# A new first stage for a gated-convolution layer: the first token tile ahead of the second, ScalarE for the second tile's tokens, and a hand-set order for a few loads and low parts

## The chip, the core and the metric

The kernel runs on one core of one Trainium2 chip. The metric is the device time of one execution in microseconds (us). Five engines work beside each other and meet through semaphores: TensorE (PE in the profile; its weight loads are listed apart as PEld) multiplies matrices, VectorE (DVE) and ScalarE (ACT) do elementwise work, GpSimd (POOL) does a little of it, and SyncE (SP) issues nearly all the loads from HBM. All loads run on the core's 16 DMA engines.

## The reference

One layer of a decoder, for 256 tokens of width D = 2048, with an inner width E = 4096, all in fp32:

```python
h = rmsnorm(x, norm_g)
mod = silu(c) @ ada_w + ada_b              # (1, 3 * 2048): shift, scale, gate
shift, scale, gate = split(mod, 3)
h = h * (1 + scale) + shift
b_gate, c_gate, v, g = split(h @ w_in, 4)  # w_in is 2048 x 16384
u = causal_depthwise_conv(c_gate * v, conv_w)      # width 3
y = (b_gate * u * silu(g)) @ w_out         # w_out is 4096 x 2048
out = rmsnorm(x + gate * y, final_g)
```

The weights are read once. `w_in` is 128 MB, `w_out` 32 MB and `ada_w` 48 MB; the multiplications of `h @ w_in` and `y @ w_out` make up nearly all of TensorE's work.

## The kernel before

**Precision.** Every fp32 operand of the large products is split in two: a high part (ScalarE casts it to the matmul type, `split_hi`) and a low part (VectorE subtracts the high part from the original, `split_lo`). A product is then three matmuls: high by high, high weights by low tokens, low weights by high tokens. So every weight tile passes through ScalarE and then VectorE before TensorE can use it, and so do the tokens: `hh_[k]` and `hl_[k]` are the high and low parts of token tile k (128 of the 2048 features, by 256 tokens).

**Token tiles.** x is normalised, turned by TensorE and scaled by `norm_g` into `xs`. Tile k is then modulated with the shift and scale of its 128 features (`mod`), which need all 2048 rows of two column blocks of `ada_w`. The 16 tiles are made in 8 groups of two. The first group is made in the first stage, which is written out in a fixed order on each engine (`in_order`, lines 202 to 434). For each later group `ada_piece` loads eight pieces of two 256 KB loads each; `ada_sums` adds each piece on VectorE to a sum (line 476 for the first row block, 478 for the others); `ada_done` lets TensorE turn the sums (line 486), VectorE reduces them, and `modulate` adds the biases (line 326) and makes the tokens: `high_tokens` on ScalarE (line 330), `low_tokens` on VectorE (lines 334 and 337). Below, piece 1 to 8 are those of the second group (tiles 2 and 3).

**The first stage.** The 16 row blocks of the first group's columns are loaded (line 233) and summed partly on TensorE (blocks 1, 11, 13 and 15: `sum0` with the row block as it is) and partly on VectorE (line 415, into `gv0`); TensorE then adds `gv0` over its partitions with a column of ones (`sum0(None, ...)`), once for the shift half and once for the scale half. Row block 15 is shared: its shift half goes to TensorE, its scale half to VectorE. One VectorE instruction adds the biases for both tiles (line 420 through 326). Then the tokens: both high parts on ScalarE, tile 0's low part on VectorE (334, 337), tile 1's by ScalarE (line 429) and GpSimd (line 433). Between them stand the high and low parts of the first weights (`raw0`, two blocks of 128 x 512).

**Passes.** `part(ch, q, k0, k1, seed)` multiplies token tiles k0 to k1 with the columns of chunk ch, quarter q of `w_in` and gathers the result in a PSUM bank; ScalarE copies it to `acc` (line 518). `plan()` fixes the order of passes and pieces with a model of its own. Counting them in that order, passes 1 to 13 use token tiles 0 and 1 alone (24 matmuls each), passes 14 to 16 tiles 0 to 3 (48 each). Pass 1 uses `raw0`; passes 2 to 13 load 512 KB each and passes 14 to 16 load 1 MB each (line 540). In most passes the matmuls go block by block: high by high, high by low tokens, low by high; so the low part of the weights is needed at the third matmul.

**Order.** In the program the pieces and passes alternate: pass 2, pass 3, piece 1, pass 4, piece 2, pass 5, pass 6, piece 3, pass 7, piece 4, pass 8, piece 5, pass 9, and so on; piece 1 of the third group stands between passes 13 and 14. Behind the first stage a scheduler of the compiler sets the order on every engine and in SP's queue, from these priorities, the dependencies and the places that are free. `behind(last)` adds an edge: what is traced inside goes after the named instructions on its engine. `later(GIVE)` gives the sums a lower priority. There are three places of 2048 columns each for raw weights, high parts and low parts (a 512 KB load takes half a place), and four for pieces. Passes 6 and 7 take the place of `raw0`.

**Small loads.** The convolution's weights (`rows2`, line 585) are loaded by GpSimd's queue; the load is traced at the tenth pass and goes behind the last GpSimd instruction of the first stage (`behind(ended)`).

Of the kernel before, what the change touches and what calls it, by code (L numbers as in the profile page):

```python
# [8 lines left out]
F32 = mybir.dt.float32  # L9
F32R = mybir.dt.float32r  # L10
AF = mybir.ActivationFunctionType
ALU = mybir.AluOpType

P = 128
# [3 lines left out]
KT = D // P  # L18
# [6 lines left out]
CT = 4  # L25
NCH = 4
NS = CT * NCH
ADA = [2] * 8
# [89 lines left out]
def short_conv_layer(ctx: ExitStack, tc: tile.TileContext, x, c, norm_g, ada_w, ada_b, w_in, conv_w, w_out, final_g, out):  # L118
    nc = tc.nc
# [58 lines left out]
    @contextmanager  # L178
    def behind(last):

        traced = nc.cur_bb.bb.instructions
        n = len(traced)
        yield
        for ins in list(traced[n:]):
            if ins.engine in last:
                tc.add_manual_dep(ins, last[ins.engine], after, reason="behind")
# [13 lines left out]
    ended = {}  # L200
# [23 lines left out]
    adas = ada_w[0].rearrange("(k p) (s f) -> p k s f", p=P, s=3)  # L224
    NK0 = ADA[0]
    first_ada = []
    for n, (j, kk) in enumerate(((0, 4), (4, 4), (8, 4), (12, 2), (14, 1), (15, 1))):
        at = w_tile(("lo", "hi")[n % 2], "at0")[:, : kk * 2 * NK0 * P]
        at = at.rearrange("p (k s f) -> p k s f", k=kk, s=2)
# [11 lines left out]
    ones = const.tile([P, 1], F32, tag="ones", name="ones")  # L241
# [29 lines left out]
    bias = vec[:, KT : 3 * KT].rearrange("p (s k) -> p s k", s=2)  # L271
# [6 lines left out]
    for t in range(TT):  # L278
        for dh in range(2):
# [3 lines left out]
            else:  # L283
                nc.vector.scalar_tensor_tensor(
                    out=junk[:, t], in0=xt[t][dh], scalar=1.0, in1=xt[t][dh], op0=ALU.mult, op1=ALU.mult,
# [14 lines left out]
    def tokens(k, part):  # L300
        return (hT[:, k] if k < KB else hT2[:, k - KB])[:, part * T : (part + 1) * T]

    hh_ = [tokens(k, 0) for k in range(KT)]
    hl_ = [tokens(k, 1) for k in range(KT)]
    xs = [slot([P, CT, T], f"xs{j}") for j in range(KT // CT)]
# [15 lines left out]
    mod = const.tile([P, 2, KT], F32, tag="mod", name="mod")  # L321

    def add_biases(k0, nk, sums):
        ks = slice(k0, k0 + nk)
        sums = sums.rearrange("p (s k) -> p s k", s=2)
        nc.vector.tensor_tensor(out=mod[:, :, ks], in0=sums, in1=bias[:, :, ks], op=ALU.add)

    def high_tokens(k):
        hf = xs[k // CT][:, k % CT, :]
        nc.scalar.activation(hh_[k], hf, AF.Identity, bias=mod[:, 0, k : k + 1], scale=mod[:, 1, k : k + 1])  # L330

    def low_tokens(k):
        hf = xs[k // CT][:, k % CT, :]
        nc.vector.tensor_scalar(
            out=hf, in0=hf, scalar1=mod[:, 1, k : k + 1], scalar2=mod[:, 0, k : k + 1], op0=ALU.mult, op1=ALU.add
        )
        nc.vector.tensor_tensor(out=hl_[k], in0=hf, in1=hh_[k].bitcast(F32), op=ALU.subtract)

    def modulate(k0, nk, sums):

        add_biases(k0, nk, sums)
        for k in range(k0, k0 + nk):
            high_tokens(k)
            low_tokens(k)

    last_low = [None]

    def hi_tile():
        return w_tile("hi", "hi", F32R)
# [4 lines left out]
    def split_hi(raw, n, hi=None):  # L354
        hi = hi_tile() if hi is None else hi
        nc.scalar.copy(hi[:, :n], raw[:, :n])  # L356
        return hi

    def split_lo(raw, n, hi, lo_tag="lo", lo=None):
        lo = lo_tile(lo_tag) if lo is None else lo  # L360
        last_low[0] = nc.vector.tensor_tensor(  # L361
            out=lo[:, :n], in0=raw[:, :n], in1=hi[:, :n].bitcast(F32), op=ALU.subtract
        )
        return hi, lo
# [19 lines left out]
    sums0 = psum.tile([P, 512], F32, tag="sm", name="sum0", bufs=2)  # L384
    gv0 = adap.tile([P, 2, 2 * P], F32, tag="gv", name="gv0")[:, :, 0 : NK0 * P]
    for dh in range(2):
        for t in range(TT):
            nc.scalar.activation(xt[t][dh], xt[t][dh], AF.Copy, scale=rstd[:, t : t + 1])
    def sum0(k, rows, col, halves=(0, 1)):


        for o in range(2 * NK0):
            if o // NK0 in halves:
                nc.tensor.matmul(
                    sums0[:, o * P : (o + 1) * P], rows[:, o // NK0, (o % NK0) * P : (o % NK0 + 1) * P],
                    col.to_broadcast([P, P]),
                    start=k == ON_PE[0] and o == 0, stop=k is None, skip_group_check=True,
                )

    for k in range(KT):  # L400
        c_k = silu_c[:, k : k + 1]
        at, gv = first_ada[k], gv0
        if k in ON_PE:
            if k == 11:
                for j in range(3):
                    keep_x(j, turn_x(j))
                tp_3 = turn_x(3)
            sum0(k, at, c_k, (0,) if k == KT - 1 else (0, 1))
            if k < KT - 1:
                continue  # L410
            at, gv = at[:, 1], gv0[:, 1]
        if k == 0:
            nc.vector.tensor_scalar_mul(gv, at, c_k)
        else:
            nc.vector.scalar_tensor_tensor(out=gv, in0=at, scalar=c_k, in1=gv, op0=ALU.mult, op1=ALU.add)
    for half in range(2):
        sum0(None, gv0, ones[:, 0:1], (half,))
    blocks0 = [raw0[:, k * CT * P : (k + 1) * CT * P] for k in range(NK0)]
    hi0 = [split_hi(b, CT * P) for b in blocks0]
    add_biases(0, NK0, sums0.rearrange("p (o f) -> p o f", o=2 * NK0)[:, :, 0])  # L420
    pieces0 = []
    for k in range(NK0):
        high_tokens(k)
    for k in range(NK0):
        if k == 0:
            pieces0.append(split_lo(blocks0[k], CT * P, hi0[k]))
            low_tokens(k)
        else:
            nc.scalar.activation(
                xs[0][:, k, :], xs[0][:, k, :], AF.Identity, bias=mod[:, 0, k : k + 1], scale=mod[:, 1, k : k + 1]  # L430
            )
            pieces0.append(split_lo(blocks0[k], CT * P, hi0[k]))
            nc.gpsimd.tensor_tensor(out=hl_[k], in0=xs[0][:, k, :], in1=hh_[k].bitcast(F32), op=ALU.subtract)
    pinned.close()

    def conv(ct, u, cv):
# [17 lines left out]
    def ada_piece(k0, nk, piece):  # L454
        w = nk * P
        kk = ASLOT // (2 * w)
        if piece == 0:
            sums[k0] = adap.tile([P, 2, 2 * P], F32, tag="gv", name="gv")
        gv = sums[k0][:, :, 0:w]
        j = piece * kk  # L460
        at = adap.tile([P, ASLOT], F32, tag="at", name="at", bufs=4)
        at4 = at.rearrange("p (k s f) -> p k s f", k=kk, s=2)
        for s in range(2):
            nc.sync.dma_start(at4[:, :, s, :], adas[:, j : j + kk, s, k0 * P : k0 * P + w])  # L464
        with later(GIVE):
            ada_sums(j, kk, at4, gv)
        if j + kk == KT:
            with later(-LEAD):
                ada_done(k0, nk, gv)
# [39 lines left out]
            product(bank[:, m, :], hi[:, o], lo[:, o], k, i, begins and i == 0, m % 2 == 0, 2 in parts and k == k1 - 1 and (m, i) == terms[-1])  # L509

    last_mm = [None]
    kept, added = [], []

    def keep(ch, q, k0, bank, seed=False):
        if k0 == 0 or seed:
# [6 lines left out]
    def part(ch, q, k0, k1, seed):  # L522


        col = q * E + ch * CT * P
        step = SLOT // (CT * P)
        first = k0
        bank = psum.tile([P, CT, T], F32, tag="mm", name="mm_s")
        if seed:
            nc.scalar.copy(bank, acc[ch, q])  # L530
        if pieces0:
            for k in range(NK0):
                chunk_products(bank, *pieces0[k], 0, k, k0, k1, late=True)
            pieces0.clear()
            k0 = NK0
        for s0 in range(k0, k1, step):
            sk = min(step, k1 - s0)
            n = sk * CT * P
            raw, hi, lo = places(n)
            nc.sync.dma_start(  # L540
                raw[:, :n].rearrange("p (k f) -> p k f", k=sk),
                w_in[0, s0 * P : (s0 + sk) * P, col : col + CT * P].rearrange("(k p) f -> p k f", p=P),
            )
            at = len(acc) if k0 == 0 else KT
            with behind(ended if at < 3 else kept[at - 3] if at < 9 else {}):
                split_hi(raw, n, hi)
            with behind(ended if at < 3 else added[at - 3] if at < 5 else {}):
                split_lo(raw, n, hi, lo=lo)
            for parts in ((0, 1), (2,)) if 0 < len(acc) < 3 else ((0, 1, 2),):
                for i in range(sk):  # L550
                    chunk_products(bank, hi, lo, i * CT * P, s0 + i, k0, k1, seed, parts=parts)
        if len(acc) == 1:
            with behind(ended):
                keep_x(3, tp_3)
        keep(ch, q, first, bank, seed)
        kept.append({ins.engine: ins.name for ins in nc.cur_bb.bb.instructions[-1:]})
# [109 lines left out]
    for ct in range(NS, NCT, 2):  # L666
        for q in QUARTERS:
            bank = psum.tile([P, CT, T], F32, tag="mm", name="mm_b")[:, 0:2]
            col = q * E + ct * P
            for kp in range(0, KT, KP):  # L670
# [6 lines left out]
                for m in range(2):  # L677
                    for i in range(KP):
                        k = kp + i
                        o = slice((i * 2 + m) * P, (i * 2 + m + 1) * P)  # L680
# [174 lines left out]
    halves = [wide_bank("mm_o") for _ in range(2)]  # L855
# [89 lines left out]
```

## Time and profile before

| | |
|---|---|
| median of 3 runs | 903.15 us (902.76 to 903.26) |
| the profiled execution | 903.37 us, of which 901.6 us are the span of its instructions |
| granted TensorE clock, mean | 0.997 |
| HBM read, written | 224.49 MB, 2.10 MB |
| TensorE's matmuls | 6997 |

A row of the timeline gives the start and the busy time in us, the engine, the line of the kernel, the operation, "output<-inputs" with their shapes, and how many of them were merged; in square brackets stands the idle time of the engine before it and what ended that. A "q" behind an engine marks its queue: a row of SPq is the issue of a load, and the transfer lands some us later. Windows give the busy time of each engine in a stretch, then the granted clock, the mean share of the 16 DMA engines that was busy (it can exceed 1, since a packet's time counts in full where packets overlap) and the GB/s.

### The profile page before, as it was taken

How to read it: one execution, taken by the hardware profiler on the slowest of the kernel's cores; microseconds unless marked ns; L12 is line 12 of the kernel's file. 1: busy time of each engine (PE TensorE's matmuls, PEld its weight loads, DVE VectorE, ACT ScalarE, POOL GpSimd, SP SyncE). 2: the span in 40 equal slices, each digit the busy share in tenths (PEclk: the TensorE clock that was granted, in tenths of full speed). 3: DMA queues.
4: the chain of work that ended last, by engine and by line, in shares of the span. 5: the costliest groups of instructions: out<-in, count | busy, mean ns of one | idle time of the engine just before them, and what ended most of it. 6: DMA issues, size and time to landing. Idle time of an engine off the chain costs nothing.

```text
span 901.6 us, 16416 instructions
## 1 busy us (share of the span) xinstructions
PE 887.4 (98%) x6997; PEld 850.6 (94%) x6997; DVE 675.3 (75%) x665; ACT 484.9 (54%) x429; POOL 84.8 (9%) x96
## 2 busy tenths in 40 slices
PE   7999999999999999999999999999999999999996
PEld 4899999999999999999999999999999988888885
DVE  5889989888888867765775678565555568879886
ACT  6768866665548856644443434444434445554543
POOL 0000000000000042024224302420000000000000
PEclk9999999999999999999999999999999999999998
DMA  9999999999998588687978898866666476673662
GB/s 307 365 369 368 368 315 348 356 369 352 351 326 289 165 277 250 192 257 229 295 227 247 256 289 269 240 198 197 201 193 188 141 284 222 199 275 123 203 234 94
DMA packets 159610, 235.01 MB, mean 261 GB/s; under 512 B 6900, under 2 KB 105284, under 8 KB 159152
## 3 DMA queue, kind: packets, MB, share of 16 engines
q1 hardware_dynamic: 156368, 226.52, 76.7%
q0 software_dynamic: 3040, 7.39, 2.8%
q8 instruction: 55, 0.90, 0.4%
q14 instruction: 19, 0.16, 0.1%
q10 hardware_dynamic: 128, 0.04, 0.0%
HBM read 224.49 MB, written 2.10 MB: 251 GB/s over the span
## 4 chain that ended last, share of the span: by engine, by line
PE 95%; DMA 3%; SPq 0%; ACT 0%; DVE 0%; issue 0%; ACTq 0%; DVEq 0%
PE mm_b L496 39%; PE mm_s L496 37%; PE mm_w L738 7%; PE mm_o L738 7%; PE mm L738 4%; DMA at<-in_ada_w_dram 2%; DMA x<-in_x_dram 1%; PE tp_g L486 0%; DVE lo L361 0%; SPq L464 0%; ACT hi L356 0%; ACT acc L518 0%; SPq L540 0%; SPq L218 0%; ACT big L852 0%
## 5 line engine op out<-in xcount | busy, mean ns | idle before, releaser
L496 PE MATMUL mm_s<-hT,hi 128*128 128x256 f32 x2048 | 348.4, 277 | 1.1 <-ACT hT L330 1.1
L496 PE MATMUL mm_b<-hT,hi 128*128 128x256 f32 x2048 | 348.2, 276 | 0.0
L496 PEld LDWEIGHTS mm_s<-hT,hi 128*128 128x128 f32 x2048 | 307.2, 188 | 1.3 <-ACT hT L330 1.3
L496 PEld LDWEIGHTS mm_b<-hT,hi 128*128 128x128 f32 x2048 | 308.2, 188 | 0.0
L496 PE MATMUL mm_b<-hT,lo 128*128 128x256 f32 x1024 | 282.8, 276 | 0.0
L496 PE MATMUL mm_s<-hT,lo 128*128 128x256 f32 x1024 | 280.2, 277 | 0.8 <-DVE lo L361 0.8
L356 ACT CAST hi<-raw 128x2048 fp32r<-128x2048 f32 (+1 forms) x66 | 123.7, 1875 | 193.5 <-PE mm_b L496 156.7
L361 DVE TENSOR_TENSOR lo<-raw,hi 128x2048 fp32r<-128x2048 f32 (+1 forms) x66 | 150.4, 2280 | 99.9 <-ACT hi L356 99.3
L496 PEld LDWEIGHTS mm_b<-hT,lo 128*128 128x128 f32 x1024 | 192.2, 188 | 0.0
L496 PEld LDWEIGHTS mm_s<-hT,lo 128*128 128x128 f32 x1024 | 190.7, 188 | 1.2 <-DVE lo L361 1.2
L361 DVE TENSOR_TENSOR lo<-raw_s,hi 128x2048 fp32r<-128x2048 f32 (+1 forms) x80 | 149.5, 1877 | 35.1 <-ACT hi L356 34.6
L356 ACT CAST hi<-raw_s 128x2048 fp32r<-128x2048 f32 (+1 forms) x80 | 124.2, 1558 | 58.2 <-PE mm_s L496 47.2
L478 DVE SCALAR_TENSOR_TENSOR gv<-at,silu_c,gv 128x512 f32<-128x512 f32 x105 | 78.5, 748 | 7.6 <-DMA at<-in_ada_w_dram 5.9
L518 ACT COPY acc<-mm_s 128x1024 f32<-128x1024 f32 x54 | 54.7, 1013 | 39.4 <-PE mm_s L496 39.2
L361 DVE TENSOR_TENSOR lo<-raw_o,hi 128x2048 fp32r<-128x2048 f32 x22 | 50.4, 2290 | 23.4 <-ACT hi L356 23.4
L356 ACT CAST hi<-raw_o 128x2048 fp32r<-128x2048 f32 x22 | 42.0, 1908 | 46.4 <-PE mm_w L738 12.6
L738 PE MATMUL mm_w<-hi,y 128*128 128x512 f32 x184 | 58.8, 389 | 0.0
L634 POOL TENSOR_TENSOR gacc<-gacc,z 128x512 f32<-128x512 f32 x28 | 44.7, 1597 | 116.2 <-DMA z<-gacc 116.2
L738 PE MATMUL mm_o<-hi,y 128*128 128x512 f32 x176 | 55.3, 389 | 0.0
L628 DVE SCALAR_TENSOR_TENSOR gacc<-at_g,silu_c,gacc 128x512 f32<-128x512 f32 x60 | 45.8, 764 | 8.2 <-DMA at_g<-in_ada_w_dram 7.2
L632 POOL DMA_DIRECT2D z<-gacc x28 | 15.6, 556 | 330.5 <-DVE acc L569 283.9
L738 PEld LDWEIGHTS mm_w<-hi,y 128*128 128x128 f32 x184 | 34.5, 188 | 7.2
(154 smaller groups left out, 689.4 us busy)
## 6 DMA issues: line engine op xcount, KB each, us to landing
raw<-in_sc_w_in_dram SPq DMA_DIRECT2D x64, 1024.0 KB, 5.8
raw_s<-in_sc_w_in_dram SPq DMA_DIRECT2D x47, 1024.0 KB, 8.3
raw_o<-in_sc_w_out_dram SPq DMA_DIRECT2D x32, 1024.0 KB, 5.3
at<-in_ada_w_dram SPq DMA_DIRECT2D x126, 256.0 KB, 7.9
raw_s<-in_sc_w_in_dram SPq DMA_DIRECT2D x33, 512.0 KB, 7.2
at_g<-in_ada_w_dram SPq DMA_DIRECT2D x32, 512.0 KB, 8.1
x<-in_x_dram SPq DMA_DIRECT2D x4, 512.0 KB, 6.3
big<-in_x_dram SPq DMA_DIRECT2D x2, 1024.0 KB, 8.2
```

Of the source, the lines that this page charges most:

```text
L356: nc.scalar.copy(hi[:, :n], raw[:, :n])
L361: last_low[0] = nc.vector.tensor_tensor(out=lo[:, :n], in0=raw[:, :n], in1=hi[:, :n].bitcast(F32), op=ALU.subtract)
L478: nc.vector.scalar_tensor_tensor(out=gv, in0=at4[:, i], scalar=c_k, in1=gv, op0=ALU.mult, op1=ALU.add)
L496: mm = last_mm[0] = nc.tensor.matmul(dst, w, h[k], start=begins and left, stop=ends, skip_group_check=True)
L518: nc.scalar.copy(acc[ch, q], bank)
L628: nc.vector.scalar_tensor_tensor(out=ga, in0=at3[:, i, :], scalar=s, in1=ga, op0=ALU.mult, op1=ALU.add)
L632: nc.gpsimd.dma_start(turned[0 : P - away], ga[away:P])
L634: nc.gpsimd.tensor_tensor(out=ga, in0=ga, in1=turned, op=ALU.add)
L738: nc.tensor.matmul(dst, y[a], b, start=opens and i == 0, stop=ends and i == 2, skip_group_check=True)
```

## The change

There are four edits.

1. The shared row block 15 of the first stage is divided by token tile and no longer by shift and scale: TensorE takes tile 0's part of both, VectorE tile 1's. `sum0` gets a list of tiles in place of halves, the sums with ones are made tile by tile, and the biases are added tile by tile (`first_bias`).
2. The tokens of the first group: tile 0's high part is made by VectorE, in one instruction that follows its bias; tile 0's float tokens, and both of tile 1's forms, by ScalarE (`first_tokens`); both low parts by VectorE. GpSimd makes none. The casts and low parts of the first weights alternate with them, tile by tile.
3. The loads of piece 3 go behind the load of pass 6, those of piece 4 behind the load of pass 7 (`loads`).
4. The low part of pass 14 goes behind the biases of the second group, the low part of pass 15 behind the last low part of that group's tokens (`made`).

```diff
     def modulate(k0, nk, sums):
 
         add_biases(k0, nk, sums)
+        made.append({ins.engine: ins.name for ins in nc.cur_bb.bb.instructions[-1:]})
         for k in range(k0, k0 + nk):
             high_tokens(k)
             low_tokens(k)
+        made.append({ins.engine: ins.name for ins in nc.cur_bb.bb.instructions[-1:]})
...
-    def sum0(k, rows, col, halves=(0, 1)):
+    def sum0(k, rows, col, tiles=range(NK0)):
...
-            if o // NK0 in halves:
+            if o % NK0 in tiles:
...
-            sum0(k, at, c_k, (0,) if k == KT - 1 else (0, 1))
+            sum0(k, at, c_k, (0,) if k == KT - 1 else range(NK0))
             if k < KT - 1:
                 continue
-            at, gv = at[:, 1], gv0[:, 1]
+            at, gv = at[:, :, P : NK0 * P], gv0[:, :, P : NK0 * P]
...
-    for half in range(2):
-        sum0(None, gv0, ones[:, 0:1], (half,))
     blocks0 = [raw0[:, k * CT * P : (k + 1) * CT * P] for k in range(NK0)]
-    hi0 = [split_hi(b, CT * P) for b in blocks0]
-    add_biases(0, NK0, sums0.rearrange("p (o f) -> p o f", o=2 * NK0)[:, :, 0])
+    hi0 = []
+
+    def first_bias(k):
+        sum0(None, gv0, ones[:, 0:1], (k,))
+        both = sums0.rearrange("p (s k f) -> p s k f", s=2, k=NK0)[:, :, k, 0]
+        nc.vector.tensor_tensor(out=mod[:, :, k], in0=both, in1=bias[:, :, k], op=ALU.add)
+
+    def first_tokens(k, out):
+        nc.scalar.activation(out, xs[0][:, k, :], AF.Identity, bias=mod[:, 0, k : k + 1], scale=mod[:, 1, k : k + 1])
+
     pieces0 = []
+    first_bias(0)
+    nc.vector.tensor_scalar(
+        out=hh_[0], in0=xs[0][:, 0, :], scalar1=mod[:, 1, 0:1], scalar2=mod[:, 0, 0:1], op0=ALU.mult, op1=ALU.add
+    )
     for k in range(NK0):
-        high_tokens(k)
-    for k in range(NK0):
-        if k == 0:
-            pieces0.append(split_lo(blocks0[k], CT * P, hi0[k]))
-            low_tokens(k)
-        else:
-            nc.scalar.activation(
-                xs[0][:, k, :], xs[0][:, k, :], AF.Identity, bias=mod[:, 0, k : k + 1], scale=mod[:, 1, k : k + 1]
-            )
-            pieces0.append(split_lo(blocks0[k], CT * P, hi0[k]))
-            nc.gpsimd.tensor_tensor(out=hl_[k], in0=xs[0][:, k, :], in1=hh_[k].bitcast(F32), op=ALU.subtract)
+        hi0.append(split_hi(blocks0[k], CT * P))
+        if k:
+            first_tokens(k, hh_[k])
+        first_tokens(k, xs[0][:, k, :])
+        pieces0.append(split_lo(blocks0[k], CT * P, hi0[k]))
+        if k + 1 < NK0:
+            first_bias(k + 1)
+        nc.vector.tensor_tensor(out=hl_[k], in0=xs[0][:, k, :], in1=hh_[k].bitcast(F32), op=ALU.subtract)
...
         for s in range(2):
-            nc.sync.dma_start(at4[:, :, s, :], adas[:, j : j + kk, s, k0 * P : k0 * P + w])
+            with behind(loads[piece + 2] if k0 == ADA[0] and piece in (2, 3) else {}):
+                nc.sync.dma_start(at4[:, :, s, :], adas[:, j : j + kk, s, k0 * P : k0 * P + w])
...
+            loads.append({ins.engine: ins.name for ins in nc.cur_bb.bb.instructions[-1:]})
             at = len(acc) if k0 == 0 else KT
             with behind(ended if at < 3 else kept[at - 3] if at < 9 else {}):
                 split_hi(raw, n, hi)
-            with behind(ended if at < 3 else added[at - 3] if at < 5 else {}):
+            with behind(ended if at < 3 else added[at - 3] if at < 5 else made[at - 13] if 13 <= at < 15 else {}):
                 split_lo(raw, n, hi, lo=lo)
```

More of the change, by code (lines that the diff above doesn't have):

```diff
@@ L344, in modulate @@
             low_tokens(k)
-    last_low = [None]
+        made.append({ins.engine: ins.name for ins in nc.cur_bb.bb.instructions[-1:]})
+    last_low, made = [None], []
     def hi_tile():
@@ L511, in short_conv_layer @@
     last_mm = [None]
-    kept, added = [], []
+    kept, added, loads = [], [], []
     def keep(ch, q, k0, bank, seed=False):
```

## The prediction

> **What bounds the kernel now.** I read the page's head first, then windows cut by stage, then the chain of waits.
>
> ```profile
> span 901.6 us, 16416 instructions
> PE 887.4 (98%) x6997; PEld 850.6 (94%) x6997; DVE 675.3 (75%) x665; ACT 484.9 (54%) x429; POOL 84.8 (9%) x96
> ```
>
> ```profile
> 9.00:25.00 16.00, 14.08 (x81) 9.94 (x79) 12.94 (x24) 10.70 (x21) 0.00 (x0) 1.00 1.07 353
> 25.00:42.00 17.00, 16.19 (x137) 15.80 (x138) 14.05 (x17) 14.16 (x18) 1.53 (x2) 1.00 1.06 363
> 42.00:62.00 20.00, 20.00 (x179) 20.00 (x178) 17.60 (x20) 14.86 (x16) 0.00 (x0) 1.00 1.07 369
> ```
>
> TensorE is the bound of the kernel as a whole (98%), so a gain can only come from where it is not yet full: up to 42 us. In the windows it is full from 42 us on, while the DMA engines are already full from 9 us (shares 1.07, 1.06, 1.07). So the start is a race between a stream of bytes of fixed length and TensorE, and what a load can bring forward depends on where it stands in that stream.
>
> ```profile
> 23.91 8.01 DMA at<-in_ada_w_dram
> ...
> 32.71 1.23 DVE lo L361
> ...
> 36.80 1.02 ACT acc L518
> 37.88 1.06 ACT hi L356
> 38.97 1.24 DVE lo L361
> ...
> 57.17 10.79 PE mm_s L496 x95
> ```
>
> ```profile
> 33.33 0.39 PE L496 MATMUL mm_s<-hT,hi 128*128 128x256 f32 x2
> 33.98 0.39 PE L496 MATMUL mm_s<-hT,lo 128*128 128x256 f32 x1 [0.27 <-DVE lo L361]
> ...
> 39.33 0.39 PE L496 MATMUL mm_s<-hT,hi 128*128 128x256 f32 x2
> 40.24 0.39 PE L496 MATMUL mm_s<-hT,lo 128*128 128x256 f32 x1 [0.53 <-DVE lo L361]
> ...
> 62.36 0.39 PE L496 MATMUL mm_s<-hT,hi 128*128 128x256 f32 x2
> 62.59 0.28 PE L496 MATMUL mm_s<-hT,lo 128*128 128x256 f32 x1
> ```
>
> The chain that ends last does not pass through the first products at all: it runs over a load of piece 2 (23.91), a low part (32.71), a copy, a cast and a low part (36.80 to 40.2), and from there over TensorE alone. TensorE's pace is 10.79/95 = 0.114 us a matmul. Two stalls stand behind the first product. In pass 4 (from 33.33) two matmuls take 0.23 and the third comes after 0.65: 0.42 lost; in pass 6 (39.33 to 40.24) 0.68 is lost. Each costs 0.1 more in refilling, so 0.5 and 0.8. With what the first product can gain, that is all there is to win. Pass 14 (62.36 to 62.59) runs at full pace; I come back to it.
>
> **Edits 1 and 2, the first stage.** Its rows:
>
> ```profile
> 21.11 2.06 DVE L415 SCALAR_TENSOR_TENSOR gv<-at,silu_c,gv 128x512 f32<-128x512 f32 x3 [0.45 <-DMA at<-in_ada_w_dram]
> 22.70 1.23 PE L394 MATMUL sum<-ones,gv 128*128 128x128 f32 x8
> 23.10 1.36 ACT L356 CAST hi<-raw 128x512 fp32r<-128x512 f32 x2 [1.72 <-DVE gv L415]
> 23.97 0.16 DVE L326 TENSOR_TENSOR mod<-sum,vec 128x4 f32<-128x4 f32 x1 [0.80 <-PE sum L394]
> 24.05 0.69 DVE L361 TENSOR_TENSOR lo<-raw,hi 128x512 fp32r<-128x512 f32 x1
> 24.36 1.09 ACT L330 ACTIVATE hT<-xs,mod 128x256 fp32r<-128x256 f32 x2
> 24.99 0.41 DVE L334 TENSOR_SCALAR xs<-xs,mod 128x256 f32<-128x256 f32 x1 [0.25 <-ACT hT L330]
> 25.44 0.42 DVE L337 TENSOR_TENSOR hT<-xs,hT 128x256 fp32r<-128x256 f32 x1
> 25.48 0.60 ACT L429 ACTIVATE xs<-xs,mod 128x256 f32<-128x256 f32 x1
> 25.01 0.74 PE L496 MATMUL mm_s<-hT,hi 128*128 128x256 f32 x4 [1.08 <-ACT hT L330]
> 27.43 2.43 PE L496 MATMUL mm_s<-hT,hi 128*128 128x256 f32 x20
> ```
>
> Now eight matmul records (1.23) end before one bias (0.16), ScalarE's 0.6 follows, and the product starts at 25.01. After the change four records for tile 0, about 0.7, come first. They start at 22.70 if they need only the sums through block 14, or at 23.2, when VectorE's last sum ends (21.11 + 2.06), if block 15's other columns hold them back: no row shows such interleaved columns. So they end at 23.4 to 23.9, the bias at 23.6 to 24.05. The high part on VectorE has no row either: the nearest is the same operation to fp32, 0.41; ScalarE's 0.60 is the upper end. First product: 24.1 to 24.7, thus 0.3 to 0.9 earlier. The matmuls for tile 1's bias stand ahead of the products on TensorE, but run while VectorE makes that high part.
>
> What counts is the end of pass 1. The first four of the 20 matmuls at 27.43 are its last ones (high weights by tile 1's low tokens, up to now from GpSimd). Afterwards ScalarE has, from the first bias on (23.85 to 24.3 with the 0.2 that it now takes to follow the bias): one token form (0.60), a cast (0.68), two forms (1.09), done at 26.2 to 26.7; VectorE has the high part, a low part (0.69), the bias, 0.42, 0.69 and is done with these by 26.1 to 26.5, and waits for ScalarE. The last low tokens (0.42) are ready at 26.7 to 27.15, against 27.43: **0.3 to 0.7 earlier**. VectorE's extra 0.42 and 0.16 lie in this wait; without it they would push the low part of pass 2 back by 0.6.
>
> GpSimd is now empty in the first stage, and that moves one load that the diff does not name:
>
> ```profile
> 27.02 0.68 POOL L585 DMA_DIRECT2D rows<-in_sc_conv_w_dram  x1
> ```
>
> It stood behind GpSimd's low tokens and can now go as soon as its tile is free, into the stretch from 9 to 25 us. 48 KB at 353 GB/s are 0.14 us in front of the first group's last row blocks. [...] I take 0.14 off: pass 1 ends about 0.35 earlier (bounds 0.15 and 0.7).
>
> **Whether that survives pass 4.**
>
> ```profile
> 32.04 0.75 DVE L478 SCALAR_TENSOR_TENSOR gv<-at,silu_c,gv 128x512 f32<-128x512 f32 x1 [1.44 <-DMA at<-in_ada_w_dram]
> ```
>
> VectorE sits here for 1.44 us on piece 2, with pass 4's low part queued behind it (32.71). The edits leave the stream's order up to there as it is. If VectorE's order stays too, TensorE's third matmul of pass 4 is still at 33.98, and the 0.35 is spent as a longer stall. With the low part ahead of that sum, 0.35 and 0.5 are kept. I take 0.
>
> **Edit 3, the loads.**
>
> ```profile
> 25.31 3.60 SPq L464 DMA_DIRECT2D at<-in_ada_w_dram  x4
> 30.50 3.33 SPq L540 DMA_DIRECT2D raw_s<-in_sc_w_in_dram  x4
> ```
>
> ```profile
> raw_s<-in_sc_w_in_dram SPq DMA_DIRECT2D x1, 512.0 KB, 9.0
> at<-in_ada_w_dram SPq DMA_DIRECT2D x1, 256.0 KB, 8.2
> raw_s<-in_sc_w_in_dram SPq DMA_DIRECT2D x1, 512.0 KB, 7.3
> ```
>
> The second fence holds, one window each, pass 5's load (issued 24.43, landing 33.4), the last of piece 4 (28.28, landing 36.5) and pass 6's (30.50, landing 37.8). Four loads of 256 KB, 1 MB, thus take 36.5 - 33.4 = 3.1 us, and pass 6's takes 1.3. Moved ahead of the four, it lands at 34.7; pass 7's at 36.1, or at 37.6 if piece 3 goes between; the pieces' last load at 39.2, so **2.7 later**. Both weights wait in SP's queue for the place of `raw0`, until about 26.3 where the pieces went at 25.31; SP's later loads wait with them, which costs nothing because 8 to 9 us of transfers are under way. Without that cover it would be 1 us of the stream.
>
> With data at 34.7 ScalarE can cast pass 6 before its copy at 36.80 (which waits for TensorE's end of pass 4), the low part ends near 38, and the 0.8 is gone. TensorE then runs 0.8 ahead from pass 6 to pass 13 (bounds 0 and 1.7).
>
> **The cap.** What is late next is pass 14:
>
> ```profile
> 57.96 1.92 ACT L356 CAST hi<-raw_s 128x2048 fp32r<-128x2048 f32 x1 [0.29 <-DMA raw_s<-in_sc_w_in_dram]
> 59.41 0.75 DVE L478 SCALAR_TENSOR_TENSOR gv<-at,silu_c,gv 128x512 f32<-128x512 f32 x1 [0.79 <-DMA at<-in_ada_w_dram]
> 60.08 2.29 DVE L361 TENSOR_TENSOR lo<-raw_s,hi 128x2048 fp32r<-128x2048 f32 x1
> 63.60 0.75 DVE L337 TENSOR_TENSOR hT<-xs,hT 128x256 fp32r<-128x256 f32 x2
> 46.38 1.96 SPq L464 DMA_DIRECT2D at<-in_ada_w_dram  x2
> ```
>
> Its cast starts when its load lands (57.9), VectorE follows, and the low part ends at 62.37; TensorE takes it at 62.59. The margin is 0.2, or 0.35 if VectorE does not first do the sum at 59.41. Edit 3 only swaps bytes that all stand ahead of this load, in a stream that is full, so it lands when it did. Whatever TensorE is ahead above 0.2 to 0.35 becomes a wait at pass 14. Behind it the slack is kept to the end, since TensorE is full.
>
> **Edit 4** costs nothing as long as the orders it asks for are those that stand there: the biases (before the sum at 59.41) precede 60.08, the last low tokens (64.35) precede the low part of pass 15. Without that cover it is the fourth rival.
>
> **Sum.** Against the profiled execution's 903.37 (span 901.6 and 1.8 around it): first stage -0.35, spent at pass 4 (0); pass 6 -0.8; given back at pass 14 +0.55: -0.25, so 903.1. The profiled run lies 0.2 above the median of 903.15, so against that: **902.9**. 0.2% (1.8 us) is about what a measurement of this kernel can tell from no change.
>
> **The rivals.** *The swap does not reach TensorE*: the copy at 36.80 stays ahead of pass 6's cast, which then cannot start before 37.88 however early the data is; gain 0, 903.15. For it: that is the present order. Against: the scheduler chose it when the data came at 37.8.
>
> *The cap lifts*: third group's piece 1 (SP, 46.38) goes behind pass 14's weights, which then land two 256 KB loads, about 1.5, earlier (half of the 3.1 for four). The cap becomes 1.7 to 1.85, and 0.35 + 0.5 + 0.8 up to 0.7 + 0.5 + 0.8 are there to fill it: 901.3. For it: pass 14's place comes free with a low part that follows TensorE, so it moves forward when TensorE does, while that piece's place does not. Against: the piece stands first in the program.
>
> *The sums hold up pass 6*, slower: VectorE keeps the four sums of pieces 3 and 4 ahead of pass 6's low part. Piece 4 lands at 39.2, its two sums end at 40.75 (2 x 0.75), the low part 1.24 later, at 42.0 and not at 40.2: +1.8, 905.0. It decides from a landing later than 38.97 - 1.5 = 37.5. Nothing takes it back, as TensorE is the bound from there. Where the following groups' sums inherit it, up to 906.
>
> *The delay reaches the second group*, slower: its sums end 2.7 later. Then edit 4 makes pass 14's low part wait for biases at about 61.3; it ends at 63.6, TensorE loses 1.1 at pass 14: 904.2, or up to 905.5 if pass 15 waits for its tokens as well. Against: piece 5 and the later ones keep their place in the stream.
>
> **How the numbers follow.** Capped at pass 14: 0.30, its own range 902.5 to 903.3. Swap without effect: 0.08. Cap lifted: 0.27. Sums ahead of pass 6: 0.23. Second group late: 0.12. Below 901.34 lies a little over half of the third case: 0.16. Above 904.96 lie three quarters of the fourth, 0.17, and 0.07 of the last: 0.24. Between: 0.60. The range reaches down to 901.0 (nearly all of the cap lifted, 0.08 left out) and up to 906.0 (0.1 left out).
>
> **What would show it.** First product between 24.1 and 24.7; the third matmul of pass 4 still at 34.0 behind the sum of piece 2; no stall at pass 6, its cast ahead of the copy; a new stall before pass 14's third matmul, its cast starting at 57.9. I am wrong if pass 14's load lands a microsecond earlier, if TensorE waits at pass 6 behind a sum, or if a stall stands beyond 75 us.

## The result, and the profile after

The changed kernel takes 905.89 us (median of 10 runs, 904.43 to 907.37); the kernel before, timed beside it, 903.38 (902.76 to 904.13). The ratio is 1.0028, 95% interval 1.0019 to 1.0037: **slower** by 2.5 us. The forecast was 902.9, so the sign was missed; 905.89 lies just inside the range. The profiled execution below took 907.37, the longest of the ten.

The windows by stage of the changed kernel (columns: window; its length, then busy time and count of PE, PEld, DVE, ACT and POOL; granted clock; DMA share; GB/s), and below them the third and fourth of the kernel before:

```profile
25.00:42.00 17.00, 16.64 (x141) 16.33 (x141) 14.16 (x18) 14.40 (x19) 0.00 (x0) 1.00 1.07 368
42.00:61.60 19.60, 19.60 (x176) 19.60 (x175) 15.12 (x20) 13.66 (x13) 0.00 (x0) 1.00 1.07 371
61.60:64.80 3.20, 1.33 (x11) 1.13 (x10) 3.20 (x4) 3.01 (x4) 0.00 (x0) 0.99 1.06 371
64.80:68.20 3.40, 3.40 (x18) 3.40 (x17) 3.40 (x5) 2.69 (x2) 0.00 (x0) 0.51 1.08 364
```

```profile
61.60:64.80 3.20, 3.20 (x31) 3.20 (x30) 3.20 (x7) 2.41 (x3) 0.00 (x0) 1.00 1.07 370
64.80:68.20 3.40, 3.40 (x32) 3.40 (x32) 2.99 (x3) 0.78 (x2) 0.00 (x0) 1.00 1.07 371
```

Up to 61.6 us TensorE does as well as before or better (16.64 busy against 16.19 in the second stage). Then come two rows that look different in the kernel before. From 61.6 to 64.8 TensorE is busy for 1.33 of 3.20 us. From 64.8 to 68.2 it looks full (3.40 of 3.40), but does 18 matmuls where the kernel before does 32: the granted clock is 0.51. "Busy" at half clock is a loss that only the clock column and the count show.

TensorE's timeline, and the chain of waits:

```profile
24.34 0.71 PE L508 MATMUL mm_s<-hT,hi 128*128 128x256 f32 x4
...
33.99 0.39 PE L508 MATMUL mm_s<-hT,lo 128*128 128x256 f32 x1 [0.36 <-DVE lo L363]
...
59.53 0.60 PE L498 MATMUL tp_g<-ident,gv 128*128 128x128 f32 x4
...
63.85 0.38 PE L508 MATMUL mm_s<-hT,lo 128*128 128x256 f32 x1 [1.87 <-DVE lo L363]
...
64.83 0.63 PE L508 MATMUL mm_s<-hT,hi 128*128 128x256 f32 x2
...
65.47 0.63 PE L508 MATMUL mm_s<-hT,hi 128*128 128x256 f32 x2
```

```profile
32.72 1.23 DVE lo L363
33.99 25.70 PE mm_s L508 x224
61.59 2.21 DVE lo L363
63.85 7.36 PE mm_s L508 x48
```

The first product comes 0.67 us earlier than before (24.34 against 25.01), and pass 4's third matmul, behind the same sum, at the same 33.99. The chain then runs over TensorE alone from 33.99 on, without the stop at pass 6, until 61.59. There it turns into a low part on VectorE, pass 14's: its third matmul starts at 63.85, and the idle time before it is 1.87. Behind it, 48 matmuls take 7.36 us, 0.153 each instead of 0.114. From 64.83 to 65.47 three take 0.64, thus 0.21 each.

VectorE around that low part, after and before (L490 and L478 are the sums, L326 the biases, L363 and L361 the low parts of weights):

```profile
52.43 1.23 DVE L363 TENSOR_TENSOR lo<-raw_s,hi 128x1024 fp32r<-128x1024 f32 x1 [0.83 <-ACT hi L358]
53.57 0.74 DVE L490 SCALAR_TENSOR_TENSOR gv<-at,silu_c,gv 128x512 f32<-128x512 f32 x1
55.15 1.23 DVE L363 TENSOR_TENSOR lo<-raw_s,hi 128x1024 fp32r<-128x1024 f32 x1 [0.83 <-ACT hi L358]
56.29 0.74 DVE L490 SCALAR_TENSOR_TENSOR gv<-at,silu_c,gv 128x512 f32<-128x512 f32 x1
...
60.17 0.69 DVE L499 TENSOR_REDUCE gs<-tp_g 128x4 f32<-128x512 f32 x1 [1.52 <-PE tp_g L498]
...
61.44 0.16 DVE L326 TENSOR_TENSOR mod<-gs,vec 128x4 f32<-128x4 f32 x1
61.51 2.29 DVE L363 TENSOR_TENSOR lo<-raw_s,hi 128x2048 fp32r<-128x2048 f32 x1
```

```profile
51.64 2.32 DVE L478 SCALAR_TENSOR_TENSOR gv<-at,silu_c,gv 128x512 f32<-128x512 f32 x3
...
57.75 0.68 DVE L487 TENSOR_REDUCE gs<-tp_g 128x4 f32<-128x512 f32 x1
58.46 0.16 DVE L326 TENSOR_TENSOR mod<-gs,vec 128x4 f32<-128x4 f32 x1
```

The second group's last sum ends at 57.03 (56.29 + 0.74) and not at 53.96; its four transposes, which stand at a fixed place in TensorE's program (here behind 298 matmuls of products, before behind 265), run at 59.53 and not at 56.58; the biases come at 61.44 and not at 58.46. All are 3 us late. Pass 14's weights are not the reason:

```profile
56.78 1.92 ACT L358 CAST hi<-raw_s 128x2048 fp32r<-128x2048 f32 x1
```

Their cast is done at 58.70, 1.2 earlier than before, and the low part waits 2.8 us behind the biases, as edit 4 asks. The sums are late by two things. On VectorE the last one stands behind the low part of pass 13 (55.15); by e5 below, which changes that order and no load's, this is 2.1 of the 3.1 us (the last sum ends there at 54.92). The rest begins in SP's queue, after and before (piece 8 in the changed kernel is the group of two at 44.22):

```profile
40.42 1.70 SPq L476 DMA_DIRECT2D at<-in_ada_w_dram  x2
42.56 1.57 SPq L552 DMA_DIRECT2D raw_s<-in_sc_w_in_dram  x2
44.22 0.93 SPq L476 DMA_DIRECT2D at<-in_ada_w_dram  x2
46.03 0.37 SPq L552 DMA_DIRECT2D raw_s<-in_sc_w_in_dram  x1
47.43 3.17 SPq L476 DMA_DIRECT2D at<-in_ada_w_dram  x4
```

```profile
40.58 3.16 SPq L464 DMA_DIRECT2D at<-in_ada_w_dram  x4
44.19 2.09 SPq L540 DMA_DIRECT2D raw_s<-in_sc_w_in_dram  x2
```

Before, pieces 7 and 8 go one behind the other (four loads at 40.58), then the weights of passes 12 and 13. Now those weights (42.56) stand between the two pieces; pieces 5 to 7 have kept their turn. Piece 8 takes the place that piece 4 leaves, and piece 4's last sum ends at 41.51 and not at 38.81:

```profile
39.98 1.53 DVE L490 SCALAR_TENSOR_TENSOR gv<-at,silu_c,gv 128x512 f32<-128x512 f32 x2
```

```profile
35.70 3.11 DVE L478 SCALAR_TENSOR_TENSOR gv<-at,silu_c,gv 128x512 f32<-128x512 f32 x4
```

(35.70 + 3.11 = 38.81, four sums of pieces 3 and 4 in a row.) That is edit 3's delay of 2.7 us. But in the run piece 8 does not wait for this place: it is free 1.0 us before the first of the two weights is issued, and 2.7 before piece 8 is. Piece 8 waits for its turn, which the compiler's scheduler has fixed. That the scheduler put it back because it, too, reckons with a later end of piece 4 fits the way in which it sets the order, but no run shows its reckoning. The last of piece 8 lands at 53.08 instead of 50.96. The same rows show that the third group's piece 1 (47.43) went behind pass 14's weights (46.03), which landed at 55.80 instead of 57.88.

### The profile page after: what moved, and what is told of

Read it like the earlier page. It is cut to its first block, busy times and chain, and to the rows that moved or that the text cites. A ratio compares the mean times of both kernels' runs of the same rounds, so it can differ in the third digit from the quotient of the medians.

```text
span 905.6 us, 16414 instructions
## 1 busy us (share of the span) xinstructions
PE 890.0 (98%) x6997; PEld 852.6 (94%) x6997; DVE 675.2 (75%) x667; ACT 483.5 (53%) x429; POOL 90.2 (10%) x95
## 4 chain that ended last, share of the span: by engine, by line
PE 93%; DMA 4%; DVE 1%; issue 1%; ACT 1%; SPq 0%; ACTq 0%; DVEq 0%
PE mm_b L508 38%; PE mm_s L508 38%; PE mm_w L751 7%; PE mm_o L751 6%; PE mm L751 4%; DMA at<-in_ada_w_dram 2%; DMA x<-in_x_dram 1%; DMA raw_o<-in_sc_w_out_dram 1%; DVE lo L363 0%; PE tp_g L498 0%; ACT hi L358 0%; DVE lo L782 0%; ACT hi L779 0%; SPq L476 0%; DVE sums_o L774 0%
## 5 line engine op out<-in xcount | busy, mean ns | idle before, releaser
L363 DVE TENSOR_TENSOR lo<-raw,hi 128x2048 fp32r<-128x2048 f32 (+1 forms) x66 | 153.1, 2321 | 100.2 <-ACT hi L358 99.8
L363 DVE TENSOR_TENSOR lo<-raw_s,hi 128x2048 fp32r<-128x2048 f32 (+1 forms) x80 | 149.8, 1875 | 42.9 <-ACT hi L358 42.4
L490 DVE SCALAR_TENSOR_TENSOR gv<-at,silu_c,gv 128x512 f32<-128x512 f32 x105 | 78.6, 749 | 3.8 <-DMA at<-in_ada_w_dram 2.2
L363 DVE TENSOR_TENSOR lo<-raw_o,hi 128x2048 fp32r<-128x2048 f32 x22 | 50.4, 2291 | 23.6 <-ACT hi L358 23.6
L647 POOL TENSOR_TENSOR gacc<-gacc,z 128x512 f32<-128x512 f32 x28 | 49.5, 1768 | 121.3 <-DMA z<-gacc 121.3
```

What stands on the lines that cost most here:

```text
L363: last_low[0] = nc.vector.tensor_tensor(out=lo[:, :n], in0=raw[:, :n], in1=hi[:, :n].bitcast(F32), op=ALU.subtract)
L490: nc.vector.scalar_tensor_tensor(out=gv, in0=at4[:, i], scalar=c_k, in1=gv, op0=ALU.mult, op1=ALU.add)
L647: nc.gpsimd.tensor_tensor(out=ga, in0=ga, in1=turned, op=ALU.add)
```

## The experiments

Starts of five matmuls of the first part, in us of each profile (1st; 97th, the first of pass 5; 313th, the first of pass 14; 505th, the first of pass 19 in the program's order; 1201st, past all that is spoken of here), with the medians and, against the kernel before timed beside each, the intervals of the ratio. The rows are explained one by one below; the 18 extra matmuls of one run are not counted in its numbering.

| kernel | median, ratio (95%) | 1st | 97th | 313th | 505th | 1201st |
|---|---|---|---|---|---|---|
| before | 903.38 | 25.01 | 36.60 | 62.36 | 84.37 | 164.73 |
| after | 905.89, 1.0019 to 1.0037 | 24.34 | 36.63 | 61.59 | 87.28 | 167.62 |
| e1 front alone | 903.30, 0.9991 to 1.0009 | 24.40 | 36.65 | 62.27 | 84.31 | 164.67 |
| e2 without edit 4 | 904.99, 1.0014 to 1.0033 | 24.51 | 36.20 | 61.18 | 85.57 | 165.92 |
| e3 edits 3, 4 alone | 905.65, 1.0013 to 1.0031 | 24.97 | 37.02 | 61.99 | 86.05 | 166.39 |
| e4 edit 3 alone | 905.30, 1.0010 to 1.0030 | 24.88 | 35.91 | 60.88 | 86.89 | 167.24 |
| e5 sum ahead | 905.39, 1.0013 to 1.0031 | 24.31 | 36.45 | 61.39 | 84.18 | 166.24 |
| e6 pass 13's load held | 903.70, 0.9997 to 1.0014 | 24.13 | 36.54 | 61.48 | 84.45 | 164.81 |
| e7 extra matmuls | 904.39, 1.0005 to 1.0022 | 24.26 | 35.83 | 62.94 | 84.86 | 165.20 |
| e8 three orders | 904.46, 1.0007 to 1.0024 | 24.32 | 35.75 | 60.72 | 83.18 | 165.20 |
| e9 e8, old front | 904.21, 1.0003 to 1.0021 | 24.85 | 35.86 | 60.80 | 83.05 | 165.09 |
| e10 e6, order at pass 4 | 903.48, 0.9993 to 1.0011 | 24.43 | 35.85 | 60.97 | 84.17 | 164.53 |
| e11 e8, earlier biases | 904.24, 1.0002 to 1.0019 | 24.33 | 35.74 | 60.71 | 83.13 | 165.62 |

The 97th starts near 36.6 or near 35.8 even where the program up to it is the same (after and e7): piece 2's load lands at 31.9 in the one profile and at 31.1 in the other, and pass 4's low part stands behind its sum. That much, 0.8, is chance of an execution.

### Which edit costs: e1 to e4

e1 takes edits 3 and 4 out of the changed kernel, e2 edit 4; e3 puts edits 3 and 4 into the kernel before, e4 edit 3 alone. Edit 4 alone was not run: the orders that it asks for already stand in the kernel before, so it is argued, and not shown, that alone it would change nothing.

```diff
-            with behind(loads[piece + 2] if k0 == ADA[0] and piece in (2, 3) else {}):
+            with behind({}):
...
-            with behind(ended if at < 3 else added[at - 3] if at < 5 else made[at - 13] if 13 <= at < 15 else {}):
+            with behind(ended if at < 3 else added[at - 3] if at < 5 else {}):
```

> The changed kernel without edits 3 and 4: the new first stage alone. Theory A (the loss comes from edits 3 and 4 together, the front is spent at pass 4): first product at about 24.3, third matmul of pass 4 still at 34.0, pass 6 keeps its stall of 0.7 us, no stall over 0.5 us at pass 14, clock 1.00 throughout; 902.9 to 903.4 us. Rival B (the new front itself does harm further on, by the orders that it brings with it): 904.5 to 906.

Measured 903.30: the front alone is neither gain nor loss. First product 24.40, 97th at 36.65 as before; pass 6 keeps its stall, and from the 313th on TensorE is where it was. Theory A held here.

> The changed kernel without edit 4: front and order of loads as changed, the low part of pass 14 free to go ahead of the second group's biases. Theory A (the wait that edit 4 asks for is the loss, with the half clock that follows it): the low part of pass 14 ends near 61.0, before TensorE asks for it at 61.7, no stall of 2 us there, no stretch at half clock; 902.0 to 902.8. Rival C (the second group is late by edit 3 and the wait only moves from the low part to that group's tokens): a stall of 1.5 to 2.5 us stands at pass 14 or 15 before products of row block 2, and 904.5 to 906.

Measured 904.99: theory A missed and **rival C held**, in its time and in its cause. VectorE and TensorE of e2:

```profile
58.30 2.29 DVE L363 TENSOR_TENSOR lo<-raw_s,hi 128x2048 fp32r<-128x2048 f32 x1 [0.66 <-ACT hi L358]
...
62.43 0.15 DVE L326 TENSOR_TENSOR mod<-gs,vec 128x4 f32<-128x4 f32 x1
...
64.24 2.29 DVE L363 TENSOR_TENSOR lo<-raw_s,hi 128x2048 fp32r<-128x2048 f32 x1
...
67.75 0.76 DVE L337 TENSOR_TENSOR hT<-xs,hT 128x256 fp32r<-128x256 f32 x2
```

```profile
66.58 0.39 PE L508 MATMUL mm_s<-hT,lo 128*128 128x256 f32 x1 [1.45 <-DVE lo L363]
```

Pass 14's low part now runs from 58.30, and its first two row blocks don't wait. But the pass takes four row blocks, and the last two need the tokens that the late biases make (their low parts only at 67.75). TensorE goes over to pass 15, and stands for 1.45 us before that pass's low part (64.24 to 66.53), not before the products of row block 2, as rival C had it. The wait only changed its place.

> The kernel before with edits 3 and 4 and the old front. Theory A: as the changed kernel, a stall of about 2 us at pass 14 behind the second group's biases and a stretch of 3.4 us at half clock behind it; 905.3 to 906.5. Rival B (the front does the harm): no such stall, 902.5 to 903.2.

Measured 905.65, with the old front: the same stall (start to start 2.13, at 64.23). Its 11 runs fall into five of 904.36 to 905.16 and six of 905.65 to 906.09; the profiled one, of the first set, shows the stall but no half clock behind it. The mean granted clock of each run agrees: 0.998 in the five, 0.996 or 0.997 in the six. So the half clock follows the same stall in some executions only.

> The kernel before with edit 3 alone. Theory A: the stall at pass 6 is gone, the low part of pass 14 is made ahead of the biases; 902.0 to 902.9. Rival C (late second group holds TensorE through its tokens): 904.5 to 906. Rival D (the order of the loads alone costs the stream): a stall ahead of pass 14.

Measured 905.30: the gain at pass 6 is there (60.88 at the 313th, 1.5 ahead of before, of which 0.7 stood at the 97th already), and is lost as in e2. Rival C again. Thus **edit 3 alone makes the loss**, and edit 4 neither makes nor mends it.

### Why the second group is late: e5 and e6

e5 puts one order on VectorE; e6 instead holds one load.

```diff
-... else made[at - 13] if 13 <= at < 15 else {}):
+... else made[at - 13] if 13 <= at < 15 else added[7] if at == 12 else {}):
                 split_lo(raw, n, hi, lo=lo)
```

> The changed kernel with one more order on VectorE: the low part of pass 13 goes behind the second group's last sum. No load moves ahead of piece 8. Theory C (the second group is late, and half of that is its last sum standing behind low parts on VectorE): the last sum starts near 53.9 instead of 56.3 us, its transposes stand 9 matmuls earlier in TensorE's program, the biases come at 59.5 to 60.3 instead of 61.4, the stall at pass 14 shrinks from 2.15 to 0.8 or less and no half clock follows; 902.6 to 903.6. Rival E (only the arrival of piece 8 at 53.1 counts): stall still over 1.5 us, 905 to 906.

The early part came as theory C had it: biases at 59.97, a stall of 0.87 at pass 14, no half clock, and the 505th matmul at 84.18, 0.2 ahead of before. But the time is 905.39. A new stall of 1.66 (start to start) stands at 138.61, before the low part of a much later pass; I come back to it with e8. It makes 1.5 of the 2.1 us (the 1201st is that far behind); the rest of the median's loss I can't place.

```diff
+            with behind(pieces[7] if len(acc) == 12 and k0 == 0 else {}):
                 nc.sync.dma_start(
                     raw[:, :n]...
```

> The changed kernel with the load of pass 13 held behind the loads of piece 8; the last sum then stands ahead of the low part of pass 13 too, and the transposes 15 matmuls earlier in TensorE's program. Theory C: piece 8 lands about 0.7 us earlier (near 52.4), biases at 58.4 to 58.8, the low part of pass 14 runs from its cast's end at 58.7 to 61.0, no stall there and full clock; 902.0 to 902.8. Rival F (pass 13's weights are then late themselves): a stall of 0.5 us or more at pass 13, 903 to 904. Rival B (something else in the new orders holds TensorE): 905 to 906.

VectorE of e6:

```profile
53.48 1.53 DVE L491 SCALAR_TENSOR_TENSOR gv<-at,silu_c,gv 128x512 f32<-128x512 f32 x2
...
58.38 0.69 DVE L500 TENSOR_REDUCE gs<-tp_g 128x4 f32<-128x512 f32 x1 [2.09 <-PE tp_g L499]
59.10 0.16 DVE L326 TENSOR_TENSOR mod<-gs,vec 128x4 f32<-128x4 f32 x1
59.59 2.28 DVE L363 TENSOR_TENSOR lo<-raw_s,hi 128x2048 fp32r<-128x2048 f32 x1
...
64.43 1.53 DVE L491 SCALAR_TENSOR_TENSOR gv<-at,silu_c,gv 128x512 f32<-128x512 f32 x2
65.88 2.28 DVE L363 TENSOR_TENSOR lo<-raw_s,hi 128x2048 fp32r<-128x2048 f32 x1
```

Measured 903.70, level with before (903.25 beside it): 2.1 us of the 2.5 come back with one load held and edits 1 to 4 all in place. Piece 8 lands at 51.63, 1.45 us earlier and not 0.7. The biases are at 59.10, and the stall at pass 14 is 0.33 instead of 2.15. The forecast of 902.0 to 902.8 was missed because the gain goes a pass later: pass 15's low part stands behind two sums (64.43) and ends at 68.16, and TensorE stands there for 0.72 (start to start). That it needs the sums' order and not the transfer alone is seen in e5, where they come as early (53.39) with no load moved. In both, the transposes then still stood for some 3 us in TensorE's queue (sums done at 55.0, transposes read at 58.4 in e6), behind products of passes 11 and 12.

### What the stall itself costs: e7

```diff
+            for _ in range(18 if at == 13 else 0):
+                nc.tensor.matmul(bank[:, 0, :], hh_[0][:, :P], hh_[0], start=True, stop=True, skip_group_check=True)
             for parts in ((0, 1), (2,)) if 0 < len(acc) < 3 else ((0, 1, 2),):
```

> The changed kernel with 18 more matmuls ahead of the first product of pass 14 (work of no use, 18 x 0.114 = 2.05 us), so that TensorE works where it waited. Theory (the stretch of 3.4 us at half clock is set off by the 2.15 us stall): nothing else moves, no run shows half clock behind pass 14; all runs lie between 904.0 and 905.2, median 904.5 against 905.9. Rival G (the half clock has another cause, as the load of the whole chip): runs still fall into two sets 1.5 us apart, median 905.5 to 906. If the extra matmuls end later than the low part does, their excess adds to both.

```profile
60.79 2.32 PE L563 MATMUL mm_s<-hT 128*128 128x256 f32 x18
62.94 0.40 PE L508 MATMUL mm_s<-hT,hi 128*128 128x256 f32 x2
63.18 0.28 PE L508 MATMUL mm_s<-hT,lo 128*128 128x256 f32 x1
```

Measured 904.39, all 11 runs between 903.95 and 905.11: the theory held. The biases come at 60.64, as late as in the changed kernel but for the 0.8 of chance at the 97th, and TensorE multiplies for nothing until the low part is there, so it never stands; its clock stays at 1.00, and no run's mean is under 0.997 (the changed kernel has 0.996 in seven of its ten). **Useless work in place of the stall saves 1.5 us** (905.89 - 904.39). That is the part of the loss that is half clock; the other 1.1 (904.39 - 903.25, before's median beside e7) is what the late biases cost, net of pass 6's gain.

### Whether a faster version is near: e8 to e11

e8 adds to e6 two orders on VectorE: piece 2's sums behind pass 4's low part, and those of the third group's piece 3 behind pass 15's. e9 is e8 with the old front, e10 is e8 without the order at pass 15, e11 is e8 with LEAD three times as large.

```diff
-        with later(GIVE):
+        with later(GIVE), behind(lows[2] if (k0, piece) == (ADA[0], 1) else lows[13] if k0 == ADA[0] + ADA[1] and piece == 2 else {}):
             ada_sums(j, kk, at4, gv)
...
                 split_lo(raw, n, hi, lo=lo)
+            lows.append({last_low[0].ins.engine: last_low[0].ins.name})
```

> The changed kernel with pass 13's load held behind piece 8 as before, and two orders more on VectorE: piece 2's sums behind the low part of pass 4, and the sums of the third group's piece 3 behind the low part of pass 15. Theory: what was left at pass 4 (0.98 us with the first matmul pair, about 0.6 of loss) and at pass 15 (0.72) goes, and about 0.3 stays at pass 14; 902.3 to 903.0, thus faster than the kernel before by 0.3 to 0.9. Rival (another wait follows at once, so that TensorE ends where it did): 903.4 to 904.0.

> The same orders (edits 3 and 4, pass 13's load behind piece 8, the two orders on VectorE) with the front of the kernel before. Theory (the front is worth its 0.35 us once pass 4 no longer swallows it): 0.2 to 0.5 us above the run with the new front, first product 0.6 to 0.7 later, end of pass 1 about 0.35 later. Rival (the front's gain is spent at pass 14 or 15 at the latest): the two are equal within 0.15, and so are TensorE's places from pass 16 on.

Both do early what was expected: at the 505th matmul TensorE is 1.2 to 1.3 ahead of before. Both then lose 1.66 near 137.6 us and end at 904.46 and 904.21. TensorE and ScalarE of e8 there:

```profile
135.84 0.39 PE L509 MATMUL mm_s<-hT,hi 128*128 128x256 f32 x2
137.61 0.39 PE L509 MATMUL mm_s<-hT,lo 128*128 128x256 f32 x1 [1.39 <-DVE lo L363]
```

```profile
133.32 2.87 ACT L358 CAST hi<-raw_s 128x2048 fp32r<-128x2048 f32 x2 [7.21 <-PE mm_s L509]
```

The cast waits until TensorE leaves its place (133.3), and cast and low part take 1.9 + 2.3. The two fronts are equal from the 313th matmul on to 0.13, and in the medians the old front is 0.25 ahead: the front's gain is nowhere to be seen, as the rival of e9 had it.

> The changed kernel with pass 13's load held behind piece 8 and piece 2's sums behind the low part of pass 4, without the order at pass 15; its later program is that of the run with the held load alone (median 903.70), which showed no stall near 138 us. Theory: the 0.6 at pass 4 is kept through pass 14, where 0.3 is lost; at pass 15 the low part moves forward by the same 0.6, since the sums ahead of it do, and its wait of 0.7 stays; no stall of 1.66 near 138; 902.8 to 903.3. Rival (pass 15 is set by its load's landing, not by the sums): TensorE waits there 1.3 and all is spent, 903.5 to 903.9.

> The run with three orders, with the biases and tokens of all groups asked for earlier in the program (LEAD three times as large), which moves the transposes of the sixth group and later ones forward. Theory (the stall of 1.66 near 138 us comes from how the scheduler mixes casts, sums and tokens of a later group, and not from the early orders): it goes or changes its size; without it 902.4 to 903.0. Rival (the stall comes with TensorE being 1.2 us ahead: weights of that pass wait for a place that TensorE frees): it stays at 1.5 to 1.8 and the time at 904.2 to 904.6.

e10 takes 903.48: no stall at 138, but at pass 15 it waits 0.73 as e6 does, and 0.56 at pass 14; between its theory's upper end (903.3) and its rival's lower one (903.5), and not to be told from before. e11 keeps the stall (1.66 at 137.56) and takes 904.24: its theory fell. The number agrees with the rival, but the rival's reason, that TensorE is 1.2 us ahead, does not go with e5, which was 0.2 ahead and shows the same 1.66. What sets it stays open: it goes with the later orders of e5, e8, e9 and e11, and is absent in e6 and e10. None of the versions beats the kernel before.

## Why the prediction was wrong

**Right, nearly to the digit: edits 1 and 2, and edit 3 up to pass 13.** First product 24.34 (forecast 24.1 to 24.7); the first of pass 2 at 27.56 and not 27.89, so 0.33 earlier (0.35); pass 4's third matmul at 33.99 (34.0), the front spent there, and e1 at zero. Loads of passes 6 and 7 landed at 34.65 and 37.52 (34.7; 36.1 or 37.6), the pieces' last at 39.00 (39.2). Pass 6's cast went ahead of the copy, its low part ended at 38.15 (near 38), and TensorE ran 0.8 ahead (42.86 to 42.07 at the first of pass 7). The small load that the diff does not name moved as well, from 27.02 to 10.39; no run shows the 0.14 that the forecast took off for it, only the 0.33 by which pass 1 ended earlier with the load there.

**Wrong: the cap.** "Edit 3 only swaps bytes that all stand ahead of this load ... so it lands when it did": pass 14's load landed 2.1 us earlier. The condition of the second rival, the lifted cap, came true, but without its gain.

**Wrong, and the step that failed: that the second group stays on time.** On it rested the price of edit 4, zero "as long as the orders it asks for are those that stand there". The fourth rival had the mechanism and its numbers: biases at 61.3 (61.44), low part done at 63.6 (63.80), 1.1 lost (1.26: the third matmul at 63.85 against 62.59). It was given 0.12 for one reason, "piece 5 and the later ones keep their place in the stream". Pieces 5 to 7 do, piece 8 doesn't: it went behind the weights of passes 12 and 13 and landed 2.1 us later, and with one of the two put back behind it (e6) nearly all of the loss is gone. Piece 8 uses the place of piece 4, which edit 3 puts 2.7 us back; that this is why the scheduler moved it is likely, but not shown. The prediction had the four places and the delay of 2.7, and did not ask what the scheduler would do with piece 8.

**Wrong in that rival too: its cause and its size.** It laid the wait to edit 4. By e2 and e4 the wait is there without edit 4: pass 14 lacks its tokens, and TensorE stands at pass 15 instead. And it counted the stall alone; a stretch at half clock behind it, which stands in no term of the prediction, costs 1.5 more (e7). So it is luck that 905.89 lies in the range: this rival reached up to 905.5, and the 906.0 came from the sums ahead of pass 6, which did not happen.

**The sum as it was**: -0.8 from pass 6 and 2.0 for the stall (2.15 less one matmul) make 1.2, as the 1.26 shows; the half clock adds 1.7 in the profiled execution (half of 3.41) and 1.5 in the medians: 2.7, measured 2.5. The profiled execution has 1.1 more at its end, where TensorE waits for one load of the last part (issued at 837.61, landed after 6.25 us, against 5.20 before); of the other profiles only e5's (6.52) and e2's (5.55) show such a wait, and the median, 1.5 lower, speaks for chance; it isn't laid to the change. What a measurement can tell from no change was set too high at 1.8 us: the interval here is 0.8 to either side.

## What to carry to other kernels

When a load is put back, read the whole queue behind it anew before saying that later loads keep their turn, and look first at the load that uses its buffer next (here four pieces on): that one was put back. When a wait is explained by an explicit order, ask who else waits for the same late thing; taking the order away only helps if the answer is no one. And look at the granted clock behind every new stall of TensorE: here the half clock that followed cost nearly as much again.

## What the runs showed of the hardware

A stall of 2.15 us between matmuls (1.87 of it idle) was followed, 0.87 us after its end, by TensorE at a granted clock of 0.50 from 64.72 to 68.13, 3.41 us:

```profile
64.72:68.13 3.41, 3.41 (x18) 3.41 (x18) 3.41 (x6) 2.77 (x2) 0.00 (x0) 0.50 1.08 363
```

(A window of the changed kernel.) It is not certain: e3 had a stall of 2.13 (1.85 idle), and its clock was 1.00 behind it in its profile, from 64.2 to 70. Here are windows of e4, which half clock follows, and of e2, which it does not:

```profile
61.60:64.80 3.20, 3.00 (x23) 2.45 (x21) 3.01 (x5) 3.20 (x4) 0.00 (x0) 1.00 1.06 375
64.80:68.20 3.40, 1.95 (x10) 1.91 (x10) 3.40 (x7) 2.00 (x2) 0.00 (x0) 0.73 1.06 376
66.30:69.70 3.40, 3.40 (x16) 3.40 (x17) 3.40 (x7) 1.23 (x1) 0.00 (x0) 0.51 1.06 370
```

```profile
61.60:64.80 3.20, 3.00 (x25) 2.61 (x23) 3.02 (x6) 3.20 (x4) 0.00 (x0) 1.00 1.05 373
64.80:68.20 3.40, 1.96 (x14) 1.75 (x15) 3.40 (x6) 2.29 (x2) 0.00 (x0) 1.00 1.06 377
68.20:75.00 6.80, 6.80 (x62) 6.80 (x61) 6.48 (x8) 2.81 (x4) 0.00 (x0) 1.00 1.07 366
```

TensorE is idle for 0.20 us of the first window in both, and for 1.45 (e4) and 1.44 (e2) of the second; then e4 has a clock of 0.51 from 66.30 to 69.70, and e2 one of 1.00 up to 75. Single stalls of 1.66 (start to start) near 138 us left the clock at 1.00 in the profiles of e5 (138.6 to 146) and e8 (137.6 to 145). So a stall of much the same length stands with half clock behind it and without, and what decides between the two is not shown.
